# A two-layer decoder trunk in float32 on one core: square sums and convolution products move from GpSimd to VectorE, the stick mask does without a select, and the order planner has a new table

## The chip, the cores and the metric

The kernel runs on one core of a Trainium2 chip. The core has five engines with queues of their own: TensorE (PE in the profile) multiplies matrices, VectorE (DVE) and ScalarE (ACT) work elementwise, GpSimd (POOL) does the same more slowly, and SyncE (SP) issues the DMAs. PE writes its results into PSUM, from which DVE and ACT take them; PE reads its operands from SBUF. The metric is the device time of one execution in microseconds (us), lower is better.

## The reference, cut to what matters

`x` is 512 positions by 1024 channels, `mem` 256 by 1024, all in float32. Layer 0 mixes with a gated convolution and differential attention, layer 1 with stick-breaking attention; each then attends into the memory tokens and applies a gated MLP with a width-3 convolution. Every step starts with an RMS norm.

```python
def rmsnorm(x, g):
    y = x * lax.rsqrt(jnp.mean(x * x, axis=-1, keepdims=True) + EPS)
    return y * g
for l in range(2):
    h = rmsnorm(x, norm_mix[l])
    x = x + (even_mixer(h, ...) if l % 2 == 0 else odd_mixer(h, ...))
    x = x + mem_attention(rmsnorm(x, norm_xattn[l]), rmsnorm(mem, norm_mem[l]), ...)
    x = x + conv_ffn(rmsnorm(x, norm_ffn[l]), ...)
# the gated convolution of even_mixer
y_a = a_b * causal_dwconv(a_c * a_x, conv_a)
# stick-breaking attention; strict: key before query
log_1m = where(strict, log_sigmoid(-z), 0)
tail = cumsum(log_1m, reverse) - log_1m
a = where(strict, exp(log_sigmoid(z) + tail), 0)
```

## The kernel before, in words

The residual stream lives in SBUF transposed, as eight chunks `x` of 128 channels by 512 positions. A float32 product is made of three float32r matmuls: each operand is split into a rounded part `hi` and a remainder `lo`, and hi·hi, hi·lo and lo·hi are added up in PSUM. The weights (264 slots of 128x1024) come by DMA into three `raw` buffers. For each slot ACT writes `hi` (L388) and DVE writes `lo` (L403); five pairs can wait for PE. The activations are split in the same way: for a norm, ACT writes gain·x rounded into `hs`, and DVE writes the remainder into a second `hs` with one SCALAR_TENSOR_TENSOR (L409). The norm's factor is applied after the product, when an accumulator (`acc`, three PSUM buffers) is evicted. For it ACT squares the eight chunks, the squares are added up in `nacc`, PE sums over channels by eight products with `ones`, GpSimd raises to the power -0.5 (its operand is `mhalf`), and where the factor is needed as a row, PE spreads it by four transposes and ACT copies it to `rrow`. Six of the seven additions of a norm run on GpSimd, the last on DVE. The norm of the memory tokens, once per layer, adds three times on GpSimd.

No instruction order is written by hand. Each part of the work is a Python generator (`norm_chunk`, `lin_stream`, `stick_block` and so on) that hands out one operation at a time with an estimated duration; the class `Issue` keeps a clock for every engine, takes the engine whose next operation can start earliest, and among its candidates the one of the best priority within a tolerance. The estimates (`LAT` and the durations in `act`, `tt`, `mm` and the others) thus fix the order on all engines when the program is built. On the chip every engine runs its list in that order and waits by semaphores.

At the opening, the first weights and the eight `x` chunks arrive together, PE runs 18 transposes of the identity (`warm`) and then the V product, of 96 matmuls, three accumulators at a time. In the stick stage 16 heads of four query blocks run beside the projections: PE makes the scores (`sc`), ACT two sigmoids (`gt`, `bt`, both tiles `g`), DVE a scan over `gt` with a mask (L1308), GpSimd an AFFINE_SELECT that zeroes `bt` from the diagonal on (L457), DVE their product, PE transposes it (`tr`), ACT and DVE split it into `pt`, and when four blocks are done PE multiplies with the values (`pv`). The rows `acc<-y`, `acc<-hi,hs` on PE in that stage are other products that fill it: the stick output projection and the projections of the next memory attention.

## Time and profile before

| | |
|---|---|
| median of 3 runs | 1558.18 us (1557.89 to 1559.99) |
| profiled execution | 1563.88 us, of it the span 1562.1 us |
| busy in the span | PE 1527.2, DVE 1046.4, ACT 746.1, POOL 187.0 us |
| matmuls | 7242, of them 5852 with 512 columns |
| mean granted PE clock | 0.991 |

The span runs from the first to the last instruction of the program; what lies around it is 1.8 us. Times of places below are counted from the start of the span. The profile models the end of a matmul, so a PE that is listed as busy isn't always at its full rate; the start of one matmul after another is the better measure.

### The profile page before, as it was taken

The numbers are of one execution on the slowest core, as the hardware profiler recorded it, in microseconds if no ns is written. First come the engines' busy times: TensorE is split into PE (matmuls) and PEld (weight loads), VectorE is DVE, ScalarE is ACT, GpSimd is POOL, SyncE is SP. The second block draws the span as 40 slices with busy tenths as digits, with TensorE's granted clock in tenths as the row PEclk, the third lists the DMA queues.
The fourth block names the chain that finished last, engine by engine and source line by source line (L and its number), as shares of the span: only waits on it lengthen the run. The fifth ranks groups of instructions, "written<-read, shape, count | busy, mean of one in ns | idle before, by whom it ended". The sixth has DMA issues, their size and how long they took to land.

```text
span 1562.1 us, 19206 instructions
## 1 busy us (share of the span) xinstructions
PE 1527.2 (98%) x7242; PEld 1267.3 (81%) x7242; DVE 1046.4 (67%) x1594; ACT 746.1 (48%) x1298; POOL 187.0 (12%) x242
## 2 busy tenths in 40 slices
PE   8999999999999999999999999999999999999999
PEld 7787888888788888888878778787887888888887
DVE  6688756565776467555688899765666775477443
ACT  5566436553544234323577778554544443244321
POOL 5311210200200000000312132203002000000000
PEclk9999999999999999999999999999999999999999
DMA  5212435311322333223221202351123322333222
GB/s 187 91 55 81 149 121 169 102 55 54 102 84 85 108 108 97 89 85 108 82 82 55 79 31 81 107 190 54 55 56 106 97 82 91 108 108 96 81 94 81
DMA packets 42428, 146.26 MB, mean 94 GB/s; under 512 B 4832, under 2 KB 4832, under 8 KB 42336
## 3 DMA queue, kind: packets, MB, share of 16 engines
q1 hardware_dynamic: 42336, 145.04, 29.5%
q8 instruction: 57, 0.93, 0.2%
q14 instruction: 35, 0.29, 0.1%
HBM read 142.92 MB, written 2.10 MB: 93 GB/s over the span
## 4 chain that ended last, share of the span: by engine, by line
PE 84%; DVE 9%; ACT 2%; issue 2%; POOL 2%; DMA 1%; SPq 0%; DVEq 0%; ACTq 0%; POOLq 0%
PE acc L439 75%; PE sc L439 3%; PE pv L439 3%; PE tr L443 2%; DVE hs L409 2%; DVE lo L403 2%; DVE g L1308 1%; DVE g L403 1%; POOL nacc L403 1%; DVE pt L403 1%; DMA x<-xT 1%; PE tr L439 1%; DVE x L403 1%; DVE h L403 0%; DVE sq L403 0%
## 5 line engine op out<-in xcount | busy, mean ns | idle before, releaser
L439 PE MATMUL acc<-hs,hi 128*128 128x512 f32 x1952 | 613.2, 393 | 0.2
L439 PEld LDWEIGHTS acc<-hs,hi 128*128 128x128 f32 x1952 | 366.2, 189 | 74.5 <-ACT hi L388 1.0
L388 ACT CAST hi<-raw 128x1024 fp32r<-128x1024 f32 (+1 forms) x264 | 272.0, 1036 | 243.3 <-PE acc L439 169.3
L439 PE MATMUL acc<-hs,lo 128*128 128x512 f32 x976 | 382.7, 392 | 4.4 <-DVE lo L403 4.3
L403 DVE TENSOR_TENSOR lo<-raw,hi 128x1024 fp32r<-128x1024 f32 (+1 forms) x264 | 321.2, 1228 | 60.3 <-ACT hi L388 57.4
L439 PE MATMUL acc<-hi,hs 128*128 128x512 f32 (+1 forms) x960 | 281.4, 371 | 0.7 <-ACT hs L391 0.7
L439 PEld LDWEIGHTS acc<-hs,lo 128*128 128x128 f32 x976 | 184.4, 189 | 42.8 <-DVE lo L403 5.7
L439 PE MATMUL acc<-h,hi 128*128 128x512 f32 x704 | 216.1, 389 | 0.0
L439 PEld LDWEIGHTS acc<-hi,hs 128*128 128x128 f32 x960 | 175.8, 192 | 29.2 <-ACT hs L391 1.1
L439 PE MATMUL acc<-lo,hs 128*128 128x512 f32 (+1 forms) x480 | 176.7, 369 | 4.7 <-DVE lo L403 4.7
L409 DVE SCALAR_TENSOR_TENSOR g<-c,pp,g 128x511 f32<-128x511 f32 (+1 forms) x176 | 132.0, 750 | 56.7 <-ACT g L391 53.6
L403 DVE TENSOR_TENSOR x<-x,acc 128x512 f32<-128x512 f32 x104 | 70.8, 683 | 146.5 <-PE acc L439 146.4
L439 PEld LDWEIGHTS acc<-h,hi 128*128 128x128 f32 x704 | 132.2, 188 | 27.4
L391 ACT ACTIVATE g<-c,pp 128x512 f32<-128x512 f32 x88 | 63.7, 723 | 154.3 <-DVE c L403 154.3
L439 PE MATMUL acc<-h,lo 128*128 128x512 f32 x352 | 136.4, 389 | 0.0
L403 POOL TENSOR_TENSOR nacc<-nacc,sq 128x512 f32<-128x512 f32 x36 | 57.8, 1607 | 525.0 <-ACT sq L391 475.5
L403 DVE TENSOR_TENSOR c<-acc,rrow 128x512 f32<-128x512 f32 x92 | 63.5, 690 | 70.1 <-PE acc L439 62.9
L439 PEld LDWEIGHTS acc<-lo,hs 128*128 128x128 f32 x480 | 92.3, 192 | 20.1 <-DVE lo L403 6.0
L439 PE MATMUL acc<-y,hi 128*128 128x512 f32 x256 | 82.4, 398 | 0.6 <-ACT y L388 0.6
L439 PEld LDWEIGHTS acc<-h,lo 128*128 128x128 f32 x352 | 66.1, 188 | 13.7
L403 DVE TENSOR_TENSOR g<-g,g 128x512 f32<-128x512 f32 (+2 forms) x112 | 64.4, 575 | 7.7 <-ACT g L388 1.4
L391 ACT ACTIVATE g<-sc,rq 128x128 f32<-128x128 f32 (+3 forms) x128 | 60.6, 531 | 2.9 <-PE sc L439 2.5
(158 smaller groups left out, 1631.5 us busy)
## 6 DMA issues: line engine op xcount, KB each, us to landing
raw<-wts SPq DMA_DIRECT2D x256, 512.0 KB, 4.0
x<-xT SPq DMA_DIRECT2D x16, 256.0 KB, 5.2
raw<-wts SPq DMA_DIRECT2D x8, 256.0 KB, 5.3
raw<-memT SPq DMA_DIRECT2D x4, 512.0 KB, 3.8
outT<-x SPq DMA_DIRECT2D x8, 256.0 KB, 2.0
pp<-par SPq DMA_DIRECT2D x1, 303.5 KB, 5.4
pp<-par SPq DMA_DIRECT2D x1, 4.0 KB, 1.7
```

The lines of the kernel that those rows point to most:

```text
L388: return nc.scalar.copy(out=out.ap, in_=in_.ap)
L391: return nc.scalar.activation(out=out.ap, in_=in_.ap, func=func, scale=_raw(scale), **kw)
L403: lambda: _ve(eng).tensor_tensor(out=out.ap, in0=in0.ap, in1=in1.ap, op=op))
L409: lambda: nc.vector.scalar_tensor_tensor(out=out.ap, in0=in0.ap, scalar=_raw(scalar), in1=in1.ap, op0=op0, op1=op1))
L439: lambda: nc.tensor.matmul(out.ap, lhsT.ap, rhs.ap, start=start, stop=stop))
L443: return Op("PE", 0.109, [in_, ident_v], [out], lambda: nc.tensor.transpose(out.ap, in_.ap, ident_v.ap))
L1308: lambda: nc.vector.tensor_tensor_scan(out=qv.ap, data0=gv.ap, data1=mv.ap, initial=1.0, op0=ALU.mult, op1=ALU.max))
```

## The change

All additions of squares go to DVE, in a generator of their own (`norm_sum`) with a lower priority than the splitting of the chunks. In the gated convolution the norm's row is squared once on ACT (`rrow2`) and multiplied in at the first eviction, so one product per channel block goes, and the other moves to DVE. The stick mask becomes a one on the diagonal only, with a scan that starts from 0: it is then 0 behind the diagonal, and the product with it zeroes `bt` there, so the AFFINE_SELECT goes; in its place GpSimd zeroes one column of `bt`. The warm-up becomes 22 matmuls of zeros that need no identity. The first weights are split at a higher priority than the rest, and the fourth V accumulator takes an `sc` buffer. The planner's table gets other durations, a latency for operations of one engine on its own results (`OWN`), and 0.4 us of margin for what PE reads from another engine (`SLACK`). Of the table two lines are shown.

```diff
-WARM = 18
+WARM = 22
+OWN = {"PE": 0.0, "ACT": 0.135, "DVE": 0.12, "POOL": 0.08, "SP": 0.0}
+SLACK = 0.4
+PREP_FIRST, SUM_FIRST, SUM = 0.45, 3.2, 1.5
...
     def ready(self, op):
         t = 0.0
+        slack = SLACK if op.eng == "PE" else 0.0
         for x in op.reads:
...
-                t = max(t, w if e == op.eng else w + LAT.get(e, 0.0))
+                t = max(t, w + OWN.get(e, 0.0) if e == op.eng else w + LAT.get(e, 0.0) + slack)
...
-        d = 0.213 if tiny else rhs.n() / 2400.0 + 0.0027
+        d = 0.224 if tiny else max(0.109, rhs.n() / PE_RATE + PE_FIX)
...
     def setup():
+        z = yield AL(pPT, F32R, (P, 256))
+        yield memset(z.v().f32(), 0.0)
+        F["zero"] = z
         yield memset(ident_v, 0.0)
...
-            yield tp(w[:, i % 4 * P:(i % 4 + 1) * P], ident_t)
+            yield mm(w[:, :256], F["zero"][:, :P], F["zero"][:, :256], True, True)
...
-            ps = yield AL(aACC)
+            ps = yield AL(aSC if name == "V" and m == 3 else aACC)
...
+    def norm_sum(N, k, ok):
+        yield Until(lambda: (N["x"], k) in F and ok() and N["n"] == k)
+        x = F[N["x"], k]
         if k == 0:
             acc = yield AL(pNA)
             yield act(acc, x, AF.Square)
...
-            yield tt(N["acc"], N["acc"], sq, ALU.add, eng="POOL" if k < KD - 1 else "DVE")
+            yield tt(N["acc"], N["acc"], sq, ALU.add)
...
+            spawn(norm_sum(N, k, ok), (SUM_FIRST if xname == "x0" else SUM) + k * 0.01)
...
-                yield tt(c, ps, N["rrow"], ALU.mult)
+                yield tt(c, ps, N["rrow2"], ALU.mult)
...
-                yield tt(c, c, N["rrow"], ALU.mult, eng="POOL")
                 t = yield AL(pC)
                 yield from conv3(c, "even_conv", j, 4, t)
                 free(c)
-                yield tt(t, t, N["rrow"], ALU.mult, eng="POOL")
+                yield tt(t, t, N["rrow"], ALU.mult)
...
-                    yield tt(acc, acc, sq, ALU.add, eng="POOL")
+                    yield tt(acc, acc, sq, ALU.add)
...
-        yield memset(mask, 1.0)
-        yield affine(mask, mask, pattern=[[1, S]], compare_op=ALU.is_ge, fill=0.0, base=-384, channel_multiplier=-1)
+        yield memset(mask, 0.0)
+        yield affine(mask, mask, pattern=[[1, S]], compare_op=ALU.not_equal, fill=1.0, base=-384, channel_multiplier=-1)
...
+        yield memset(bt[:, w - 1:w], 0.0)
...
-        yield Op("DVE", 0.068 + w / 960.0, [gv, mv], [qv],
-                 lambda: nc.vector.tensor_tensor_scan(out=qv.ap, data0=gv.ap, data1=mv.ap, initial=1.0, op0=ALU.mult,
+        yield Op("DVE", 0.08 + w * 0.0021, [gv, mv], [qv],
+                 lambda: nc.vector.tensor_tensor_scan(out=qv.ap, data0=gv.ap, data1=mv.ap, initial=0.0, op0=ALU.mult,
                                                       op1=ALU.max))
-        yield affine(bt[:, tsl], bt[:, tsl], pattern=[[-1, P]], compare_op=ALU.is_gt, fill=0.0, base=0,
-                     channel_multiplier=1)
...
-    spawn(prep(), 3.0)
+    spawn(prep(range(1)), PREP_FIRST)
+    spawn(prep(range(1, len(GROUPS))), 3.0)
```

The order moves on all engines. Three places matter below.

The first is DVE at the opening, from the second half of the second weight slot on. `lo` rows are weight remainders, `hs` rows remainders of the `x` chunks, `nacc` rows additions of squares. Before:

```order
L403 TENSOR_TENSOR lo_203<-raw_166,hi_202 128x512
L409 SCALAR_TENSOR_TENSOR hs_183<-x_179,pp_119,hs_182 128x512
L409 SCALAR_TENSOR_TENSOR hs_194<-x_187,pp_119,hs_193 128x512
L409 SCALAR_TENSOR_TENSOR hs_209<-x_199,pp_119,hs_208 128x512
L403 TENSOR_TENSOR lo_250<-raw_181,hi_249 128x512
L409 SCALAR_TENSOR_TENSOR hs_222<-x_214,pp_119,hs_221 128x512
```

Of the changed kernel, the same place:

```order
L411 TENSOR_TENSOR lo_224<-raw_175,hi_223 128x512
L411 TENSOR_TENSOR nacc_158<-nacc_158,y_217 128x512
L417 SCALAR_TENSOR_TENSOR hs_203<-x_198,pp_119,hs_202 128x512
L411 TENSOR_TENSOR lo_262<-raw_201,hi_261 128x512
L417 SCALAR_TENSOR_TENSOR hs_210<-x_205,pp_119,hs_209 128x512
L411 TENSOR_TENSOR lo_262<-raw_201,hi_261 128x512
L411 TENSOR_TENSOR nacc_158<-nacc_158,y_269 128x512
```

Three chunk remainders stood in a row ahead of the third slot's weight remainder; now one chunk and one half slot alternate, and the additions stand between them.

The second is DVE at the norm ahead of the first MLP (376 to 402 us in the profile), from the last but one residual addition `x<-x,acc` on. Before:

```order
L403 TENSOR_TENSOR x_1870<-x_1870,acc_3648 128x512
L409 SCALAR_TENSOR_TENSOR hs_3715<-x_1866,pp,hs_3714 128x512
L409 SCALAR_TENSOR_TENSOR hs_3727<-x_1870,pp,hs_3726 128x512
L403 TENSOR_TENSOR x_1877<-x_1877,acc_3662 128x512
L403 TENSOR_TENSOR lo_3731<-raw_3584,hi_3730 128x1024
L409 SCALAR_TENSOR_TENSOR hs_3755<-x_1877,pp,hs_3754 128x512
L403 TENSOR_TENSOR lo_3761<-raw_3596,hi_3760 128x1024
L403 TENSOR_TENSOR nacc_3680<-nacc_3680,sq_3773 128x512
```

Of the changed kernel, from the same residual addition on (the numbers of the tiles differ):

```order
L411 TENSOR_TENSOR x_1881<-x_1881,acc_3652 128x512
L411 TENSOR_TENSOR nacc_3677<-nacc_3677,sq_3716 128x512
L411 TENSOR_TENSOR lo_3726<-raw_3587,hi_3725 128x1024
L417 SCALAR_TENSOR_TENSOR hs_3733<-x_1881,pp,hs_3732 128x512
L411 TENSOR_TENSOR x_1885<-x_1885,acc_3666 128x512
L411 TENSOR_TENSOR nacc_3677<-nacc_3677,sq_3737 128x512
L411 TENSOR_TENSOR nacc_3677<-nacc_3677,sq_3766 128x512
L417 SCALAR_TENSOR_TENSOR hs_3761<-x_1885,pp,hs_3760 128x512
L411 TENSOR_TENSOR nacc_3677<-nacc_3677,sq_3772 128x512
L411 TENSOR_TENSOR nacc_3677<-nacc_3677,sq_3783 128x512
L411 TENSOR_TENSOR nacc_3677<-nacc_3677,sq_3788 128x512
L411 TENSOR_TENSOR lo_3744<-raw_3599,hi_3743 128x1024
```

The weight remainder `lo_3726` (before: `lo_3731`) has moved ahead of the last residual addition, and five additions of squares now stand between that addition and the next weight remainder.

The third is PE at the end of the stick stage, where the last head's third block is transposed (`tr<-ident,g`, three tiles). Before:

```order
L439 MATMUL acc_8703<-y_7525,lo_8466 128x512
L439 MATMUL acc_8772<-y_6731,hi_8249 128x512
L439 MATMUL acc_8772<-y_6732,hi_8249 128x512
L443 MATMUL tr_8826<-ident,g_8675 128x128 x3
L439 MATMUL acc_8772<-y_6731,lo_8250 128x512
L439 MATMUL acc_8772<-y_6936,hi_8266 128x512
```

Of the changed kernel, ahead of the same transposes:

```order
L447 MATMUL acc_8869<-hi_8858,hs_8805 128x512
L447 MATMUL acc_8869<-lo_8859,hs_8805 128x512
L447 MATMUL tr_8895<-ones,nacc_8761 128x1 x4
L447 MATMUL acc_8869<-hi_8858,hs_8806 128x512
L447 MATMUL acc_8869<-hi_8858,hs_8805 128x512
L447 MATMUL acc_8869<-lo_8859,hs_8805 128x512
L447 MATMUL acc_8869<-hi_8858,hs_8806 128x512
L451 MATMUL tr_8910<-ident,g_8702 128x128 x3
```

Between the transposes of the last head's second and third block stood 26 matmuls of the output projection; now the second block's come later, and 18 matmuls of the next memory attention and its sum of squares stand between the two.

## The prediction

> **What bounds the kernel now.** I read the page's busy shares first, then the granted clock, the waits of PE, and the table of stages.

> ```profile
> span 1562.1 us, 19206 instructions
> PE 1527.2 (98%) x7242; PEld 1267.3 (81%) x7242; DVE 1046.4 (67%) x1594; ACT 746.1 (48%) x1298; POOL 187.0 (12%) x242
> core 0: 1562.1 us, clock 0.991
> 407.26 340.06 PE acc L439 x1500
> ```

> PE bounds the kernel: the rows say 98% busy, and the last one (of the chain that ended last: start, length, what) shows what full rate is: 1500 matmuls in 340.06 us, 227 ns each, with nothing lost. The change leaves the number of products as it is, so it can only win back what PE loses. That comes in two kinds. PE is idle for 1562.1 - 1527.2 = 34.9 us, and the clock is granted at 0.991 on average, which is 0.009 x 1562.1 = 14.1 us of half clock behind longer waits. A third kind is hidden: a 512-column matmul is listed with 0.39 us though the next starts after 0.227, so every short wait loses up to 0.16 us more than its idle time.

> Where it is lost (idle = us minus PE busy; clock loss = us times 1 minus PEclk):

> ```profile
> core 0: us, PE busy (x) PEld busy (x) DVE busy (x) ACT busy (x) POOL busy (x), PEclk, DMA share, GB/s
> 0.00:26.00 26.00, 21.55 (x77) 17.15 (x78) 18.54 (x20) 15.80 (x26) 9.52 (x14) 0.93 0.66 221
> 60.00:190.00 130.00, 126.67 (x635) 104.70 (x634) 107.47 (x276) 79.59 (x192) 29.43 (x30) 1.00 0.31 91
> 270.00:300.00 30.00, 29.01 (x130) 23.52 (x130) 17.07 (x28) 16.65 (x33) 8.84 (x7) 0.94 0.24 73
> 366.00:410.00 44.00, 41.48 (x180) 33.40 (x179) 29.00 (x32) 19.75 (x27) 11.45 (x7) 0.96 0.31 96
> 410.00:748.00 338.00, 338.00 (x1493) 279.88 (x1492) 209.68 (x260) 125.62 (x156) 0.00 (x0) 1.00 0.31 97
> 764.00:860.00 96.00, 90.85 (x540) 78.14 (x539) 75.06 (x123) 67.30 (x130) 20.93 (x49) 1.00 0.21 66
> 860.00:990.00 130.00, 120.83 (x701) 101.62 (x702) 117.20 (x193) 96.57 (x193) 34.39 (x69) 1.00 0.20 62
> 990.00:1060.00 70.00, 70.00 (x313) 57.87 (x312) 43.08 (x59) 36.94 (x57) 3.50 (x5) 0.95 0.50 158
> 1060.00:1085.00 25.00, 22.55 (x96) 17.92 (x95) 18.80 (x21) 11.47 (x20) 11.71 (x8) 0.93 0.28 85
> 1165.00:1206.00 41.00, 38.79 (x162) 31.52 (x162) 27.23 (x30) 17.87 (x24) 11.45 (x7) 0.92 0.31 97
> ```

> By row, idle plus clock: opening 4.5 + 1.8 = 6.3; differential attention 3.3; first memory norm 1.0 + 1.8 = 2.8; first MLP norm 2.5 + 1.8 = 4.3; stick 5.2 + 9.2 = 14.4, and 3.5 of half clock just behind it; second memory norm 2.4 + 1.8 = 4.2; second MLP norm 2.2 + 3.3 = 5.5. Together 44.3 us. Every row that loses has POOL work in it; the first MLP (410 to 748), which has none, loses nothing.

> ```profile
> PE acc L439 <- DVE lo L403: 9.0, 5, 2.3
> PE tr L443 <- DVE pt L403: 6.8, 8, 1.3
> ```

> The waits name the same engine each time: PE waits for DVE, for weight remainders at the norms and for `pt` in the stick stage.

> **Part 1: the sums leave GpSimd.** Groups by line (busy, mean ns), then places in time (start, length):

> ```profile
> L409 DVE SCALAR_TENSOR_TENSOR hs<-x,pp,hs 128x512 fp32r<-128x512 f32 x48 | 56.3, 1216 | 4.2 <-ACT hs L391 4.2
> L403 POOL TENSOR_TENSOR nacc<-nacc,sq 128x512 f32<-128x512 f32 x36 | 57.8, 1607 | 525.0 <-ACT sq L391 475.5 <-issue 47.6
> L403 POOL TENSOR_TENSOR nacc<-nacc,y 128x512 f32<-128x512 f32 x6 | 8.7, 1456 | 9.2 <-ACT y L391 8.9
> L403 POOL TENSOR_TENSOR c<-c,rrow 128x512 f32<-128x512 f32 x8 | 11.2, 1399 | 36.5 <-DVE c L403 26.4 <-DVE c L409 8.8 <-DVE s L419 1.4
> L403 DVE TENSOR_TENSOR nacc<-nacc,sq 128x512 f32<-128x512 f32 x5 | 3.4, 682 | 1.2 <-POOL nacc L403 1.2
> L403 DVE TENSOR_TENSOR lo<-raw,hi 128x1024 fp32r<-128x1024 f32 x256 | 313.6, 1237 | 55.5 <-ACT hi L388 52.6
> ...
> 388.10 9.93 POOL L403 TENSOR_TENSOR nacc<-nacc,sq 128x512 f32<-128x512 f32 x6 [49.08 <-ACT sq L391]
> 393.51 3.39 DVE L409 SCALAR_TENSOR_TENSOR hs<-x,pp,hs 128x512 fp32r<-128x512 f32 x2 [0.19 <-ACT hs L391]
> 397.42 1.69 DVE L403 TENSOR_TENSOR lo<-raw,hi 128x1024 fp32r<-128x1024 f32 x1
> 399.04 0.74 DVE L409 SCALAR_TENSOR_TENSOR hs<-x,pp,hs 128x512 fp32r<-128x512 f32 x1
> 399.17 0.50 PE L439 MATMUL acc<-hs,lo 128*128 128x512 f32 x1 [2.14 <-DVE lo L403]
> ```

> The same `hs` remainder takes 0.74 us at 399.04, with GpSimd idle, and 1.70 at 393.51, beside its additions; the mean of all 48 is 1.216. So the additions stretch DVE by about 48 x (1.216 - 0.74) = 22.8 us in this group alone. That goes. In exchange DVE gets 42 additions and four products at 0.682: 31.4 us. DVE's total thus hardly falls; what changes is the place. Stretched remainders and weights stand ahead of PE, and the wait of 2.14 us at 399.17 is for the `lo` that had stood behind them. The additions themselves are needed only at the end of the norm.

> At the first MLP norm the order shows what is late next. Behind the last residual addition DVE does five additions, one remainder and one `lo`: 0.68 x 6 + 0.74 + 1.24 = 6.1 us with that residual addition, and 30 MLP matmuls, 30 x 0.227 = 6.8 us, stand on PE ahead of the sum of squares. So this wait closes, barely; if ACT's squares come late, 1 us stays. With the wait the half clock behind it goes. I take 3.5 of 4.3 here, 4.5 of 5.5 at the second MLP norm, 2.0 of 2.8 and 3.2 of 4.2 at the two memory norms. If the cover isn't there, the five additions cost up to 5 x 0.68 = 3.4 us a norm.

> One thing speaks against it. GpSimd keeps the power, on the way to every row factor:

> ```profile
> 283.18 1.02 POOL L403 TENSOR_TENSOR k<-s,mhalf 128x4 f32<-128x4 f32 x1 [2.11 <-DVE s L419]
> 404.61 1.94 POOL L403 TENSOR_TENSOR k<-s,mhalf 128x4 f32<-128x4 f32 x1 [6.58 <-DVE s L419]
> ```

> At 404.61 it took 0.92 us longer, while DVE worked on a `lo`. Six norms could lose 0.92 each, 5.5 us, when DVE is never idle there; two do so already, so I count 1 us inside the figures above. [...]

> The convolution's products (8 x 1.4 us of GpSimd) stand in the 130 us with 3.3 idle; with the margin of part 3 I take half, 1.6. Squaring the row costs ACT one more operation, hidden as ACT is busy for 48%. On SP one load of memory tokens has moved nine places up and holds one of three `raw` buffers longer; the waits of PE name no DMA, so I count nothing.

> **Part 2: the opening.**

> ```profile
> 12.99 5.23 DVE L409 SCALAR_TENSOR_TENSOR hs<-x,pp,hs 128x512 fp32r<-128x512 f32 x3
> 18.14 1.75 DVE L403 TENSOR_TENSOR lo<-raw,hi 128x512 fp32r<-128x512 f32 x1
> 19.94 0.50 PE L439 MATMUL acc<-lo,hs 128*128 128x512 f32 x1 [2.29 <-DVE lo L403]
> 1.40:6.26 4.86, 4.10 (x18) 3.70 (x18) 0.71 (x2) 2.07 (x4) 0.05 (x2) 1.00 0.76 242
> 6.26:10.49 4.23, 4.23 (x10) 3.36 (x11) 3.21 (x5) 3.86 (x8) 0.99 (x1) 1.00 1.00 342
> ```

> Three remainders, stretched as at 393.51 (5.23 us, 1.74 each), stood ahead of the `lo` that PE waited 2.29 us for. In the new order that `lo` comes behind one remainder and one addition, at full speed: this wait goes, and the 1.7 us of half clock behind it. The fourth V accumulator gives PE 24 more matmuls, 5.4 us, before it needs the norm. These are 4.0 us. The last row shows 10 matmuls in 4.23 us, 0.423 each: PE starts at half rate, though the clock's column has no record there. The new warm-up needs no identity, so it can start a little before 1.4 us; its 22 products of 256 columns, half of this row's 512, last 22 x 0.212 = 4.7 us and reach the first real matmul, where the old one (the row above) left a break of 0.76. That may bring full rate sooner, worth between 0 and 10 x (0.423 - 0.227) = 2.0 us; I take 0.5, near the row, where 4.1 us of transposes had not done so. Opening: 4.5.

> [...]

> **Part 3: the stick stage.**

> ```profile
> L1308 DVE TENSOR_TENSOR_SCAN g<-g,g 128x512 f32<-128x512 f32 x16 | 19.8, 1235 | 0.0
> L457 POOL TENSOR_SCALAR_AFFINE_SELECT g<-g 128x128 f32<-128x128 f32 x64 | 35.0, 548 | 125.4 <-ACT g L391 118.9 <-DVE g L403 3.4 <-PE tr L443 1.6
> 985.07 3.26 POOL L403 TENSOR_TENSOR nacc<-nacc,sq 128x512 f32<-128x512 f32 x2 [0.74 <-ACT sq L391]
> 986.13 2.47 DVE L409 SCALAR_TENSOR_TENSOR hs<-raw,pp,hs 128x256 fp32r<-128x256 f32 x2
> 989.75 0.54 PE L443 MATMUL tr<-ident,g 128*128 128x128 f32 x3 [1.94 <-DVE g L403]
> ```

> The old table gave a scan over 512 columns 0.068 + 512/960 = 0.60 us; it takes 1.235. So the planner thought `g` ready half a microsecond early, once per block, and put the transposes there. The new table says 1.16, and with 0.4 of margin PE gets other products in front. The select's 0.548 runs beside scan and sigmoid and costs little on the path; its removal saves latency, which I count at nothing, between 0 and its 0.55 a block, since the scan that runs beside it is longer where it matters (1.235 at 512 columns). The zeroed column needs only a free `bt` and stands ahead of the scores; GpSimd has time there. The 1.94 us at 989.75 is the stretch again: two remainders of 2.47 beside GpSimd's sums.

> What doesn't go is DVE's own load: 117.20 of 130 us in 860 to 990, no scan and no product less, three additions more. PE needs 120.83 busy there, so there is room, but little, and queues on an engine that is 90% busy are not what a table foresees. I keep 4 of 14.4 us and take 10.4; of the 3.5 of half clock behind, 3.0; and for the short waits' hidden 0.16 us, some 20 of them, 3.0.

> **Sum** against the profiled execution: 4.5 + 1.6 + 2.0 + 3.5 + 10.4 + 3.0 + 3.0 + 3.2 + 4.5 = 35.7 us. 1563.88 - 35.7 = 1528.2. The median of the runs, 1558.18, is 5.7 below the profiled execution, so the forecast is 1522.5 us.

> **The rivals.** *DVE stays the bound in the stick stage*: its 90% speak for it. Then the 10.4, 3.0 and 3.0 stay lost, 19.3 are saved: 1539. *All waits close*: the margin leaves 2 us of the 44.3, and hidden losses of 7 go too: 49 saved, 1509 (7: the 0.16 us for some 45 short waits); the first MLP, without a wait, shows that the planner can do it. *The additions take the place of the stretch at the norms*: they stand ahead of weight remainders in the order; then the four norms keep their 13.2 and, with powers held up, lose 5.5 more: 17 are saved, 1541. *Slower*: DVE becomes the bound, with 31.4 us added on it; if the stretch doesn't come from GpSimd's additions and stays, every added microsecond delays the remainders that PE waits for: 1558.2 + 31.4 = 1589.6. It decides once DVE has no idle time left where it gets the additions; the row of 366 to 410 has 15 us idle against 4.1 added, so this is unlikely. *The change does nothing*: waits only move, as the short ones in the order could: 1558.

> **How the numbers follow.** Forecast (1515 to 1530) 0.48; all waits close (1503 to 1515) 0.17; stick stage stays or norms stay (1530 to 1545) 0.24; less than that, but faster 0.03; nothing 0.03; slower 0.05. The predicted time is 1522. The range reaches from 1507, most of the low case, to 1543, where the two middle rivals end. A measurement of this kernel tells some 0.2% (3 us) from no change: faster 0.92, same 0.03, slower 0.05.

> **What would show it.** In the changed profile the `hs` remainders must have a mean of 0.75 us; the waits of PE for `lo` must be under 2 us in all; mean clock at 0.995 or above; no half clock at 21, 400 and 1200 us. In the stick stage, idle under 5 us, with DVE over 90% busy. PE should start real matmuls at about 6.2 us. The forecast is wrong if remainders stay at 1.2 us (then it wasn't GpSimd), if PE waits for `nacc` or `k` at the norms (additions or power late), or if PE waits for `pt` and `g` as long as before.

## The result, and the profile after

The changed kernel takes 1522.41 us (median of 4 runs, 1521.06 to 1523.14), beside 1558.04 for the kernel before in the same session (4 runs, 1554.25 to 1559.99). The ratio is 0.9773, with a 95% interval of 0.9753 to 0.9793. The forecast was 1522.0, the range 1507 to 1543. The profiled execution took 1523.14 us.

First the page's head for the changed kernel, its granted clock, and the last long piece of the chain that ended last (start, length, what):

```profile
span 1521.4 us, 19156 instructions
PE 1507.2 (99%) x7246; PEld 1261.0 (83%) x7246; DVE 1040.9 (68%) x1640; ACT 746.2 (49%) x1299; POOL 85.4 (6%) x193
core 0: 1521.4 us, clock 0.999
1167.87 349.79 PE acc L447 x1543
```

PE does the same work at the same rate (349.79 / 1543 = 0.227 us a matmul) and is idle for 14.2 us where it was idle for 34.9. DVE's total has hardly moved (1046.4 to 1040.9), though it took over 42 additions; GpSimd's fell from 187.0 to 85.4.

The table of stages of the changed kernel, in the columns of the one before (us, PE, PEld, DVE, ACT, POOL busy, PEclk, DMA share, GB/s):

```profile
6.26:10.49 4.23, 3.74 (x15) 2.68 (x16) 3.31 (x5) 3.66 (x7) 0.00 (x0) 1.00 1.01 380
0.00:26.00 26.00, 24.14 (x110) 20.29 (x111) 17.81 (x35) 16.40 (x28) 4.11 (x15) 1.00 0.75 255
60.00:190.00 130.00, 124.02 (x618) 102.58 (x617) 102.60 (x274) 76.71 (x184) 18.50 (x21) 0.99 0.27 82
190.00:250.00 60.00, 60.00 (x280) 49.80 (x279) 38.40 (x55) 29.66 (x48) 3.79 (x5) 1.00 0.44 134
380.00:400.00 20.00, 19.98 (x94) 16.41 (x94) 16.96 (x24) 10.24 (x15) 1.92 (x1) 1.00 0.23 72
750.00:850.00 100.00, 98.36 (x587) 86.08 (x587) 83.01 (x135) 72.92 (x141) 10.65 (x54) 1.00 0.23 69
850.00:970.00 120.00, 119.29 (x698) 103.29 (x697) 114.08 (x190) 95.52 (x187) 10.13 (x62) 1.00 0.24 70
970.00:1035.00 65.00, 65.00 (x305) 53.90 (x305) 45.69 (x65) 36.02 (x59) 4.33 (x5) 1.00 0.51 164
1035.00:1055.00 20.00, 19.78 (x93) 16.14 (x92) 14.00 (x22) 11.21 (x21) 3.31 (x3) 1.00 0.33 105
1150.00:1175.00 25.00, 24.98 (x117) 20.53 (x116) 19.35 (x29) 13.43 (x19) 1.92 (x1) 1.00 0.26 85
```

The first row is the start of the real products: 15 matmuls, where the kernel before made 10 in the same stretch at half rate. Read the others against the rows before, idle plus clock. Both MLP norms (380 and 1150) and the first memory norm (now near 229) lose nothing; the second (1035) loses 0.2. The stick stage (750 to 970) loses 1.6 + 0.7 instead of 14.4, with DVE at 114.08 of 120 us, 95%. One row got worse: between 60 and 190 us PE now loses 6.0 us idle and 1.3 of clock, where it lost 3.3.

Groups by line of the changed kernel (busy, mean ns of one | idle before), and what PE waits for most (us, times, longest):

```profile
L417 DVE SCALAR_TENSOR_TENSOR hs<-x,pp,hs 128x512 fp32r<-128x512 f32 x48 | 33.9, 747 | 1.6 <-ACT hs L399 1.4
L411 DVE TENSOR_TENSOR nacc<-nacc,sq 128x512 f32<-128x512 f32 x41 | 28.2, 687 | 3.1 <-ACT sq L399 1.9
L411 POOL TENSOR_TENSOR k<-s,mhalf 128x4 f32<-128x4 f32 x6 | 8.8, 1465 | 583.1 <-DVE s L427 583.1
PE tr L451 <- DVE c L411: 2.5, 2, 2.1
PE sc L447 <- DVE s L878: 1.8, 1, 1.8
```

The 48 remainders fell from 1216 to 747 ns each. PE's waits for weight remainders and for DVE's `pt` are gone; the longest left is for `c`, in differential attention.

### The profile page after: what moved, and what is told of

Its sections match the earlier page's. It is cut to its first block, busy times and chain, and to the rows that moved or that the text cites. A ratio compares the mean times of both kernels' runs of the same rounds, so it can differ in the third digit from the quotient of the medians.

```text
span 1521.4 us, 19156 instructions
## 1 busy us (share of the span) xinstructions
PE 1507.2 (99%) x7246; PEld 1261.0 (83%) x7246; DVE 1040.9 (68%) x1640; ACT 746.2 (49%) x1299; POOL 85.4 (6%) x193
## 4 chain that ended last, share of the span: by engine, by line
PE 95%; DVE 3%; ACT 1%; issue 0%; DMA 0%; POOL 0%; SPq 0%; DVEq 0%; ACTq 0%
PE acc L447 84%; PE sc L447 4%; PE pv L447 3%; PE tr L451 3%; DVE lo L411 1%; PE tr L447 1%; DMA x<-xT 0%; POOL s L411 0%; DVE h L411 0%; DVE kl L417 0%; ACT hi L396 0%; DVE c L411 0%; ACT h L396 0%; DVE sq L411 0%; DVE nacc L411 0%
## 5 line engine op out<-in xcount | busy, mean ns | idle before, releaser
L411 DVE TENSOR_TENSOR lo<-raw,hi 128x1024 fp32r<-128x1024 f32 (+1 forms) x264 | 314.9, 1205 | 59.4 <-ACT hi L396 56.5
L447 PE MATMUL acc<-hi,hs 128*128 128x512 f32 (+1 forms) x944 | 268.0, 363 | 0.8 <-ACT hs L399 0.8
L447 PEld LDWEIGHTS acc<-hi,hs 128*128 128x128 f32 x944 | 169.1, 189 | 27.4 <-ACT hs L399 1.5
L447 PE MATMUL acc<-lo,hs 128*128 128x512 f32 (+1 forms) x472 | 172.3, 365 | 0.1
L417 DVE SCALAR_TENSOR_TENSOR g<-c,pp,g 128x511 f32<-128x511 f32 (+1 forms) x176 | 132.0, 750 | 56.3 <-ACT g L399 53.2
L447 PEld LDWEIGHTS acc<-lo,hs 128*128 128x128 f32 x472 | 89.0, 189 | 13.2 <-DVE lo L411 0.2
L399 ACT ACTIVATE g<-sc,rq 128x128 f32<-128x128 f32 (+7 forms) x128 | 60.8, 536 | 2.6 <-PE sc L447 2.0
L447 PEld LDWEIGHTS acc<-y,hi 128*128 128x128 f32 x256 | 47.8, 188 | 9.5
```

What stands on the lines that cost most here:

```text
L399: return nc.scalar.activation(out=out.ap, in_=in_.ap, func=func, scale=_raw(scale), **kw)
L411: lambda: _ve(eng).tensor_tensor(out=out.ap, in0=in0.ap, in1=in1.ap, op=op))
L417: lambda: nc.vector.scalar_tensor_tensor(out=out.ap, in0=in0.ap, scalar=_raw(scalar), in1=in1.ap, op0=op0, op1=op1))
L447: lambda: nc.tensor.matmul(out.ap, lhsT.ap, rhs.ap, start=start, stop=stop))
```

## The experiments

Each kernel was timed beside runs of the kernel before on the same chip. The differences below are between medians, and those under 3 us are near what a measurement tells. The changed kernel itself was timed in another session, so a difference from its 1522.41 us also holds what the sessions differ by (the kernel before had medians of 1558.04, 1558.83, 1560.50 and 1557.15 us); the ratios, each beside the kernel before of the same session, are free of that, but have the wider spread of the kernel before in them. Twelve kernels ran: in the first nine one part is undone or done alone.

**The table alone.** The kernel before with the new scheduler table and nothing else (three of its lines are shown; the other durations of the table go with them):

```diff
+OWN = {"PE": 0.0, "ACT": 0.135, "DVE": 0.12, "POOL": 0.08, "SP": 0.0}
+SLACK = 0.4
...
-        yield Op("DVE", 0.068 + w / 960.0, [gv, mv], [qv],
+        yield Op("DVE", 0.08 + w * 0.0021, [gv, mv], [qv],
```

> The kernel before with the new scheduler table alone (traced durations, own-engine delay, margin 0.4); every operation, the select and GpSimd's sums stay. Theory 'GpSimd stretches DVE, and the stick stage suffers from the scan's short entry': the stick stage improves by some 10 to 13 us, the norms' waits stay as remainders still take about 1.2 us (mean of the 48): 1540 to 1546 us. Rival 'the table does nearly all': below 1530. Rival 'the table is worth nothing without the moved sums': 1553 to 1560.

Measured: 1544.03 us (1542.72 to 1547.39), ratio 0.9907 (0.9873 to 0.9941). Its group of remainders, and its longest entry among PE's waits:

```profile
L415 DVE SCALAR_TENSOR_TENSOR hs<-x,pp,hs 128x512 fp32r<-128x512 f32 x48 | 55.4, 1194 | 4.3 <-ACT hs L397 4.3
PE acc L445 <- DVE lo L409: 9.9, 6, 2.1
```

With GpSimd's sums in place the remainders stay at 1194 ns and PE waits for weight remainders as before. The table takes about 15 us off, and not the norms' waits.

**The work alone.** The changed kernel with the old table (the same lines the other way).

> The changed kernel with the old table (old durations, no own-engine delay, no margin); its operations, mask and opening stay. Theory 'GpSimd stretches DVE': the 48 remainders have a mean of 0.75 us, the norms' waits mostly close, the stick stage keeps its loss of some 10 to 13 us: 1535 to 1542 us. Rival 'the table does nearly all': 1550 to 1558. Rival 'operations do nearly all': below 1528.

Measured: 1533.46 us (1533.25 to 1533.73), ratio 0.9842 (0.9814 to 0.9870); its 48 remainders take 745 ns. The mechanism is the expected one; the time is 1.5 us below the range of the theory, and well above the rival's. The window of the stick stage, 764 to 990 us, in the kernel before, with the table alone, with the work alone, and with both (the changed kernel):

```profile
764.00:990.00 226.00, 211.68 (x1241) 179.76 (x1241) 192.26 (x315) 163.87 (x322) 55.32 (x118) 1.00 0.21 63
764.00:990.00 226.00, 221.15 (x1304) 191.21 (x1303) 201.74 (x329) 170.59 (x330) 56.72 (x119) 1.00 0.23 73
764.00:990.00 226.00, 215.62 (x1263) 182.63 (x1263) 200.29 (x328) 168.88 (x330) 18.77 (x103) 1.00 0.24 71
764.00:990.00 226.00, 223.65 (x1319) 194.41 (x1318) 206.15 (x338) 176.14 (x345) 19.09 (x104) 1.00 0.26 80
```

Idle of PE is 14.3, 4.9, 10.4 and 2.4 us: the stick stage needs the table first, the work second.

**One entry of the table undone.**

```diff
-        yield Op("DVE", 0.08 + w * 0.0021, [gv, mv], [qv],
+        yield Op("DVE", 0.068 + w / 960.0, [gv, mv], [qv],
```

> The changed kernel with one entry of the table as before: the scan over w columns listed with 0.068 + w/960 us (0.60 at 512, measured 1.235). Theory 'this entry was the planner's mistake in the stick stage': most of the 10 to 11 us that the old table costs as a whole come back there, 1528 to 1533 us, with PE waiting for pt and g again. Rival 'the other entries and the own-engine delay carry it': 1520 to 1525.

Measured: 1535.82 us (1534.81 to 1537.06), ratio 0.9845 (0.9822 to 0.9868), 13.4 us above the changed kernel, no less than the whole old table (11.1; by the ratios 11.2 and 10.8). The same window, and the wait that heads PE's list, as it does in the kernel with the work alone (6.4 us there):

```profile
764.00:990.00 226.00, 215.25 (x1263) 183.77 (x1262) 196.39 (x325) 167.27 (x330) 17.44 (x103) 1.00 0.22 70
PE tr L451 <- DVE pt L411: 7.6, 11, 1.1
```

Without this one number, the duration of the scan, the rest of the table gains nothing here. A run with this number alone new was not made.

**No margin.**

```diff
-SLACK = 0.4
+SLACK = 0.0
```

> The changed kernel with the margin at 0 instead of 0.4 us, traced durations kept. Theory 'the scan's duration was the planner's mistake, the margin catches only the short waits': 3 to 6 us lost, 1525 to 1528. Rival 'the margin is what keeps PE busy': 10 us or more lost, 1532 or above. Rival 'the margin is worth nothing': 1521 to 1524.

Measured: 1521.65 us (1521.40 to 1522.02), ratio 0.9766 (0.9738 to 0.9794). The last rival holds: the margin is worth nothing. That contradicts the prediction, which let the margin close short waits.

**The sums back on GpSimd.**

```diff
-            yield tt(N["acc"], N["acc"], sq, ALU.add)
+            yield tt(N["acc"], N["acc"], sq, ALU.add, eng="POOL" if k < KD - 1 else "DVE")
...
-                    yield tt(acc, acc, sq, ALU.add)
+                    yield tt(acc, acc, sq, ALU.add, eng="POOL")
```

> The changed kernel with its sums of squares back on GpSimd, as before (the last of each norm on DVE), all else as changed. Theory 'GpSimd stretches DVE': remainders return to about 1.1 us or more, PE waits for remainders at the norms again, 8 to 15 us lost: 1530 to 1538. Rival 'with the new table the place of the sums no longer matters, as the planner puts other products in front of the waits': 1520 to 1525.

Measured: 1532.79 us (1530.45 to 1534.47), ratio 0.9836 (0.9806 to 0.9866): 10.4 us lost (9.8 by the ratios).

```profile
L417 DVE SCALAR_TENSOR_TENSOR hs<-x,pp,hs 128x512 fp32r<-128x512 f32 x48 | 47.8, 1034 | 5.9 <-ACT hs L399 5.8
PE acc L447 <- DVE lo L411: 5.0, 6, 1.4
```

The remainders stretch to 1034 ns, somewhat less than expected: 14 of the 48 take more than 0.9 us, where 23 did in the kernel before. PE waits for weight remainders again. The new table, which has no entry for the stretch, didn't order around it.

**The old opening.** Old warm-up, old priorities, the fourth V accumulator in the old pool:

```diff
-            ps = yield AL(aSC if name == "V" and m == 3 else aACC)
+            ps = yield AL(aACC)
...
-PREP_FIRST, SUM_FIRST, SUM = 0.45, 3.2, 1.5
+PREP_FIRST, SUM_FIRST, SUM = 3.0, 0.5, 1.5
```

> The changed kernel with the opening as before (18 transposes of the identity as warm-up, weights prepared behind the norm's remainders, the sums of the first norm early, the fourth V accumulator in the same pool). Theory as predicted, 4.5 us: 1525.5 to 1528.5 us, full clock granted only near 10 us. Rival 'with the sums off GpSimd the opening's wait has gone by itself': 1521.5 to 1524. Rival 'the opening carries 7 us or more': 1529 and above.

Measured: 1531.30 us (1526.93 to 1534.23), ratio 0.9815 (0.9781 to 0.9849): 8.9 us lost, at the lower end of the largest rival (6.5 by the ratios, between the theory and this rival). Its DVE in the opening, and the matmul that waits (start, length; idle before and what ended it):

```profile
14.27 0.75 DVE L417 SCALAR_TENSOR_TENSOR hs<-x,pp,hs 128x512 fp32r<-128x512 f32 x1
14.94 0.68 DVE L411 TENSOR_TENSOR nacc<-nacc,y 128x512 f32<-128x512 f32 x1
15.54 0.74 DVE L417 SCALAR_TENSOR_TENSOR hs<-x,pp,hs 128x512 fp32r<-128x512 f32 x1
16.21 0.68 DVE L411 TENSOR_TENSOR nacc<-nacc,y 128x512 f32<-128x512 f32 x1
16.81 0.68 DVE L411 TENSOR_TENSOR lo<-raw,hi 128x512 fp32r<-128x512 f32 x1
...
17.55 0.79 PE L447 MATMUL acc<-lo,hs 128*128 128x512 f32 x1 [2.25 <-DVE lo L411]
```

Every row of DVE is at full speed and none is idle, yet PE waits 2.25 us: in the old order the sums, now on DVE, stand between the remainders and ahead of the `lo`. Without its reordering the opening would have traded the stretch for a queue. Not all of the 8.9 us is this: between 60 and 190 us this profile has the idle time of the changed kernel (6.0), but two stretches of 3.41 us at half clock where the changed kernel's has one:

```profile
60.00:190.00 130.00, 124.02 (x611) 102.41 (x610) 103.33 (x274) 76.52 (x185) 19.78 (x21) 0.97 0.26 81
```

**The old warm-up alone**, with the new order kept:

```diff
-            yield mm(w[:, :256], F["zero"][:, :P], F["zero"][:, :256], True, True)
+            yield tp(w[:, i % 4 * P:(i % 4 + 1) * P], ident_t)
```

> The changed kernel with the old warm-up alone (18 transposes of the identity instead of 22 products of zeros); the new order of the opening and the fourth V accumulator stay. Theory 'the warm-up without a break is what brings the full clock at 5.5 us instead of 10.5': the first 10 matmuls take 0.42 us each again, 2 us lost: 1523.5 to 1525.5. Rival 'any unbroken stretch of PE does it, the old warm-up serves as well once real products follow': 1521 to 1523. Rival 'a late start throws the order of the opening out': 1526 or above.

Measured: 1522.33 us (1521.71 to 1524.76), ratio 0.9777 (0.9756 to 0.9798): no difference, so in these runs the order and the accumulator carry the opening. The start of PE with the old opening (first two rows) and here (last two):

```profile
1.36 4.10 PE L451 MATMUL pv<-ident 128*128 128x128 f32 x18 [1.36 <-POOL mhalf L460]
6.21 0.80 PE L447 MATMUL acc<-hi,hs 128*128 128x512 f32 x1 [0.75 <-ACT hs L399]
...
1.36 3.65 PE L451 MATMUL pv<-ident 128*128 128x128 f32 x18 [1.36 <-POOL mhalf L460]
6.20 0.50 PE L447 MATMUL acc<-hi,hs 128*128 128x512 f32 x1 [1.20 <-ACT hs L399]
```

The same 18 transposes from the same 1.36 us on bring the full clock at 10.5 us in one execution and at 4.4 in the other. Of the four profiles with the old warm-up one was fast here; of the ten with the new one, all but that of the longer power (below), where the real products began 1.1 us later, at 7.31. So the early clock came more often with the new warm-up; four timed runs don't show what that is worth.

**The select back.** The old mask, no zeroed column, and

```diff
+        yield affine(bt[:, tsl], bt[:, tsl], pattern=[[-1, P]], compare_op=ALU.is_gt, fill=0.0, base=0,
+                     channel_multiplier=1)
```

> The changed kernel with the select of the stick stage back (64 of them on GpSimd, the old mask, no zeroed column). Theory 'it stood beside other work', as the prediction counted it at nothing: 1520.5 to 1525 us. Rival 'its 0.55 us stood on the path of each block, and it stretched DVE': 5 us or more lost, 1527 or above, with PE waiting for pt.

Measured: 1524.18 us (1522.58 to 1524.84), ratio 0.9768 (0.9746 to 0.9791): 1.8 us above the changed kernel by the medians, 0.8 below it by the ratios: nothing that can be told from none, as the first theory has it.

**The convolution's products back on GpSimd**, no squared row:

```diff
-                yield tt(c, ps, N["rrow2"], ALU.mult)
+                yield tt(c, ps, N["rrow"], ALU.mult)
...
+                yield tt(c, c, N["rrow"], ALU.mult, eng="POOL")
...
-                yield tt(t, t, N["rrow"], ALU.mult)
+                yield tt(t, t, N["rrow"], ALU.mult, eng="POOL")
```

> The changed kernel with the convolution's row factors as before (each c multiplied by the row twice, once on DVE and once on GpSimd, and the product t on GpSimd; no squared row). Theory 'their move was worth its 1.6 us': 1523.3 to 1526 us. Rival 'the four products more on DVE are what made differential attention worse (waits of PE between 60 and 140 us 9.6 us instead of 5.6)': 1518 to 1520.5, and those waits fall to 7 us or less. Rival 'worth nothing either way, the order of the new table is the cause': 1520.5 to 1523.3 with waits as long as now.

Measured: 1525.02 us (1524.27 to 1525.20), ratio 0.9790 (0.9771 to 0.9810): 2.6 us lost. The window from 60 to 190 us in the kernel with the table alone, with the work alone, in this one, and in the one without margin:

```profile
60.00:190.00 130.00, 122.93 (x617) 100.40 (x616) 105.19 (x271) 76.32 (x186) 32.34 (x29) 1.00 0.27 83
60.00:190.00 130.00, 126.52 (x634) 104.29 (x633) 106.27 (x278) 78.22 (x184) 16.71 (x21) 1.00 0.27 85
60.00:190.00 130.00, 122.80 (x608) 100.32 (x608) 102.65 (x264) 74.13 (x178) 30.25 (x29) 0.99 0.27 82
60.00:190.00 130.00, 125.83 (x631) 103.73 (x630) 104.95 (x276) 78.90 (x186) 15.32 (x21) 1.00 0.29 89
```

Idle is 7.1 with the new table on the old work, 3.5 with the old table on the new work, 7.2 here and 4.2 without margin, beside 6.0 in the changed kernel. So the products were not what made this stage worse; the order that the new table draws is, and as the last row shows, the margin has a part in it. Each number is of one profile.

**A longer power**, as the planner's entry for GpSimd's power, 0.36 + 0.165 x 8 = 1.68 us for 8 columns, is shorter than the 2.92 us that it took at 58.74 in the changed kernel, with DVE work beside it:

```diff
-            d = 0.36 + 0.165 * out.n()
+            d = 1.36 + 0.165 * out.n()
```

> The changed kernel with GpSimd's power listed with 1 us more (1.36 + 0.165 n), nothing else. Theory 'what is left in differential attention (9.6 us between 60 and 140 us) comes from powers that DVE holds up, 1.9 to 2.9 us instead of 1.64, which the planner does not know': 2 to 5 us saved, 1517 to 1520.5 us. Rival 'there the queue of DVE is the cause, not the power': 1521.5 to 1524, and the waits between 60 and 140 us stay at 8 us or more.

Measured: 1521.32 us (1520.95 to 1522.96), ratio 0.9754 (0.9731 to 0.9776). Inconclusive: idle between 60 and 190 us falls from 6.0 to 4.8, but the gain is too small to be told from none.

**Two candidates** with both edits, in full (margin 0, power 1 us longer) and by half (margin 0.2, power 0.5 us longer):

> A candidate: the changed kernel without margin (0) and with GpSimd's power listed 1 us longer, the two edits that measured 0.8 and 1.1 us below the changed kernel. Theory 'they take different waits': 1519.5 to 1521. Rival 'the order is drawn anew with every entry, gains of this size don't add': 1521 to 1524.

> A candidate halfway: margin 0.2, power listed 0.5 us longer. Theory 'the gain grows with either entry': about 1521, between the changed kernel and the candidate with both edits in full. Rival 'the order is drawn anew with every entry': anything from 1518 to 1525, without relation to the other two.

Measured: 1521.30 us (1520.97 to 1521.81), ratio 0.9767 (0.9747 to 0.9787), and 1520.08 (1519.61 to 1520.47), ratio 0.9759 (0.9740 to 0.9779). Gains as small as those of the two edits can't be seen to add or not. But in one session the half step is better than the full one, run for run, so the time doesn't follow the size of these entries: they draw the order anew. The second is the fastest kernel seen, 2.3 us below the changed one; its window from 60 to 190 us is idle for 3.5 us again:

```profile
60.00:190.00 130.00, 126.54 (x635) 104.50 (x634) 108.16 (x281) 79.41 (x188) 18.31 (x21) 1.00 0.28 88
```

Between 1520 and 1522 the runs don't settle which kernel is better, since the two were not timed in one session and the intervals of their ratios overlap.

## Why the prediction was right, point by point

**The parts come near the whole.** Undone one at a time from the changed kernel, they cost by the medians: sums 10.4, table 11.1, opening 8.9, convolution 2.6, select 1.8. Together 34.8 us, of the 35.6 between the medians. By the ratios they are 9.8, 10.8, 6.5, 2.6 and -0.8, 28.9 of 35.4, so the close sum is in part chance; that the sums and the table are the two large parts holds either way. The stretch and the scan's entry are two separate causes: each side of the change leaves the other's waits standing.

**The sums** were the cause named: the remainders' 0.75 us, no wait for weight remainders, no half clock at the norms, all as announced. From the rows after, the norms give 2.8, 4.3, 4.0 and 5.5 us against 2.0, 3.5, 3.2 and 4.5 predicted. The rival in which the additions take the place of the stretch was real in one place: in the opening with its old order.

**The stick stage** gives 12.1 us and the half clock behind it 3.5, against 10.4 and 3.0. The mechanism was right (the scan's entry), and of the 4 us kept for a DVE that is 95% busy 2.3 are still lost.

**The opening** was sized too small: idle plus clock fell from 6.3 to 1.9 us, and in the profiled execution full rate also came at once, worth the 2.0 us of which the prediction took 0.5. The term said 4.5; the rows give 6.4. The last 1.5 of it is luck in part: the old warm-up brought full rate as early too, in one of four profiles.

**Differential attention** was wrong in sign: 1.6 us saved were predicted, 4.0 were lost (from 3.3 to 7.3). The step that failed is "with the margin of part 3 I take half": the margin gains nothing there (without it the stage is idle for 4.2 us, not 6.0) or elsewhere, as the run without it shows. With the products back on GpSimd the stage is idle for 7.2 us, so their move by itself is worth some 1.2 us there; what the term left out is that the new order takes more from this stage than that. The largest piece, at the same place in the kernel before (first two rows) and in the changed kernel:

```profile
64.51 2.55 POOL L403 TENSOR_TENSOR s<-s,mhalf 128x8 f32<-128x8 f32 x1 [6.83 <-DVE s L419]
68.53 0.63 PE L443 MATMUL tr<-ident,c 128*128 128x128 f32 x4 [1.16 <-DVE c L403]
...
58.74 2.92 POOL L411 TENSOR_TENSOR s<-s,mhalf 128x8 f32<-128x8 f32 x1 [6.77 <-DVE s L427]
58.96 1.21 DVE L411 TENSOR_TENSOR lo<-raw,hi 128x1024 fp32r<-128x1024 f32 x1
...
61.70 0.57 DVE L427 TENSOR_SCALAR s<-s,k 128x8 f32<-128x8 f32 x1 [1.14 <-POOL s L411]
62.31 0.69 DVE L411 TENSOR_TENSOR c<-acc,s 128x512 f32<-128x512 f32 x1
...
63.14 0.78 PE L451 MATMUL tr<-ident,c 128*128 128x128 f32 x4 [2.13 <-DVE c L411]
```

In the second candidate a power of this shape took 1.64 us at 48.95, beside `h<-tr,h` on DVE. At the place shown it takes longer in both kernels, beside a `lo`: 2.55 us in the kernel before, where the `lo` had started 0.17 us ahead of it, and 2.92 here, where it started 0.22 us behind. (Being beside a `lo` isn't enough: at 56.04 in the kernel before one started 0.17 us behind a power, and the power took 1.64.) So this power was 0.91 us longer before the change too, and PE waited 1.16 us for `c`; now DVE has nothing else to do for 1.14 us, and PE waits 2.13. Of the 0.97 us more, 0.37 is the longer power; the rest is that PE's other products end 2.27 us after the start of the power (58.74 to 61.01) and not 2.86 (64.51 to 67.37). Why the new order leaves PE without other work sooner was not settled. The prediction had the price of such a power (0.92 us longer), but counted it only at the norms, where it turned out harmless: the six powers there rose from 1325 ns to 1465, and PE's weight loads wait 0.9 us in all behind them.

**The sum** was right by luck: two errors cancelled. Against the profiled execution 35.7 us were predicted and 1563.88 - 1523.14 = 40.7 came: terms short by 1.9 in the opening, 0.8 + 0.8 + 0.8 + 1.0 at the norms, 2.2 in the stick stage and behind it, and, as what is left over, about 3 in the hidden part of short waits (the rows give 34.6 of the 40.7; the hidden part itself was not measured), less 5.6 in differential attention. The other error is the step from the profiled execution to the median, 5.7 us, which was taken off on top of the sum. What it is, the timed runs show: nine runs of the kernel before on one chip, with the granted clock of each.

```
us     1553.85 1554.60 1555.75 1557.14 1557.15 1557.51 1560.29 1560.29 1561.08
clock  0.997   0.997   0.995   0.995   0.995   0.994   0.993   0.993   0.992
```

From 0.997 to 0.992 is 0.005 x 1558 = 7.8 us of half clock, and the times differ by 7.2. The profiled execution, at 0.991, was one of the unluckiest; from there to the 0.995 of the median run are 0.004 x 1558 = 6.2 us. The changed kernel's runs are at 0.999 to 1.0 and spread over 2.1 us. So the 5.7 us were, as far as these clocks tell, half clock that the sum already took away; counted twice, they made up for the 5.0 that the terms fell short.

## What to carry to other kernels

Where GpSimd works beside a chain that sets the time, price the stretch of the other engine's work too: here the 48 remainders had a mean of 1216 ns with the additions on GpSimd and of 747 without, so moving 42 additions of 0.69 us onto the busier engine left its total where it was (1046.4 and 1040.9 us) and took the waits away. In an ordering table look for the one entry that is off by the length of a wait before adding margins, and expect some luck from every redrawn order (here four small edits of the table gave 1520.1 to 1521.7 us). When a profile is turned into a sum, note first how unlucky that execution was (its granted clock beside that of the timed runs), and don't take that luck off a second time on the way to the median.

## What the runs showed of the hardware

A wait of about 2 us costs clock in one execution and not in another. Windows of the changed kernel (first two rows) and of the one with the old warm-up (last three), around the same wait of 2.13 us for `c`:

```profile
60.07:63.48 3.41, 1.28 (x8) 0.81 (x7) 2.20 (x6) 0.86 (x3) 3.22 (x5) 1.00 0.58 173
63.48:66.89 3.41, 3.41 (x11) 2.73 (x10) 1.92 (x6) 2.23 (x8) 0.74 (x3) 0.50 0.00 0
...
59.01:62.42 3.41, 2.30 (x11) 1.56 (x9) 2.23 (x4) 1.32 (x4) 3.33 (x2) 1.00 0.67 181
62.42:65.83 3.41, 2.40 (x13) 2.08 (x14) 2.74 (x7) 1.40 (x4) 1.97 (x6) 1.00 0.25 102
65.83:69.24 3.41, 3.41 (x17) 2.83 (x16) 2.08 (x6) 2.65 (x8) 0.00 (x0) 1.00 0.00 0
```
